# Attention and recurrence of a hybrid encoder layer: TensorE's order written out by the program

## The chip, the cores and the metric

The kernel runs on one core of a Trainium2 chip. The metric is the device time of one execution in microseconds (us). The core has five engines: TensorE (PE in the profile; its weight loads are listed as PEld), VectorE (DVE), ScalarE (ACT), GpSimd (POOL) and SyncE (SP, which here only issues DMA transfers). Each engine takes its own instructions strictly in the order of its queue; semaphores order the engines among each other.

## The reference

One layer of a streaming encoder over 1024 frames of width 1024, all in float32. Two mixers work on the same projection: chunked band attention (8 heads of 64) and a gated delta rule (4 heads of 128).

```python
u = rms_norm(h, mix_norm_gain);  proj = u @ w_in
aq, ak, av, dqkv, dgate, da, db = split(proj)
# A: own chunk of 64 frames and the 8 before it, QK-RMSNorm, learned bias on the distance
scores = einsum('bcqhd,bckhd->bchqk', qc, kb) * Dh**-0.5 + bias
o = einsum('bchqk,bckhd->bcqhd', softmax(scores), vb)
# B: gated DeltaNet: conv(4)+SiLU, L2-normalised q and k, chunked recurrence
t_mat = a_strict + eye(CHUNK)
value, k_cumdecay = solve(t_mat, v_beta), solve(t_mat, k_beta * exp(decay))
def step(S, inp):                          # S0 = 0
    v_new = val - kc @ S
    o = qd @ S + att @ v_new
    return S * cd + kt.T @ v_new, o
h = h + concat[rms_norm(A), rms_norm(B) * silu(dgate)] @ w_out
h = h + relu(rms_norm(h) @ w_ff1)**2 @ w_ff2
```

## The kernel before, in words

The program is written in a tile framework: it emits instructions with tiles, and a scheduler orders every engine's queue by a simulated timeline, with the order of emission as priority. Pools of tiles have a set number of buffers; a tile waits until one is free.

Stages, in order of time: projections (a 128x512 weight block times the transposed input, three passes of a split float32); attention and recurrence together; the output projection; two feed-forward products.

The recurrence works in chunks of 128 frames (NT = 8). `delta_prep` builds for each chunk the strictly lower matrix A and stores it (`a_dr`), stores `kt` for the state update, and inverts the 32x32 diagonal blocks of all chunks together by substitution on VectorE; the inverses go to `x_dr` and transposed to `y_dr`. For each chunk, `delta_merge` joins the inverted blocks: first 32 to 64 (tiles p1, p2, lines 568 and 577), then 64 to 128 (tp, p4, lines 582 to 594). `delta_state` makes the serial steps (c_tpv, c_pk, c_pv, c_pq, c_pS), `delta_out` the output within the chunk (c_Ltd, c_tpq, c_mt, c_po), `delta_fin` its transpose. The four-head products come from the helper on line 461, each float32 matmul of 128 columns as two instructions in the trace. `delta_all` deals the steps of neighbouring chunks out in the order of the string ORDER; each step ends with a `yield` of a cost.

Attention works on units (g, t, pp): a group g of four heads, a tile t of 128 queries, a pair pp of heads. A unit has up to n = 5 tiles of keys. `score` makes the products (t_sb for the last two key tiles, t_sa for the older ones, line 793) into three PSUM banks of pool ps_a, VectorE adds the bias and takes the maximum, ScalarE the exponential. `value` transposes the probabilities with PE (t_tpb line 844, then t_tpa line 855 for each of two heads) through the two banks of pool ps_t; ScalarE and VectorE copy them out (lines 847, 860, 858), and PE multiplies with the values (t_o, line 865). `finish` divides by the sums and `turn` transposes the result into `mix`.

The three generators `attention`, `delta_all` and the rest of the value projection (`values`) are dealt out by `interleave`, which always advances the one with the least work done by its weight. That sets only the order of emission, so the priority; where an instruction lands in PE's queue is the scheduler's choice, instruction by instruction.

Of the kernel before, what the change touches and what calls it, by code (L numbers as in the profile page):

```python
# [8 lines left out]
F32 = mybir.dt.float32  # L9
F32R = mybir.dt.float32r  # L10
AF = mybir.ActivationFunctionType
ALU = mybir.AluOpType
# [26 lines left out]
WARM = 8  # L39
LAST = {"b22": "t1", "t3": "t2", "t4": "b22"}  # L40
RS = "a"
NV = 6
# [4 lines left out]
def hymba_kernel(  # L47
# [60 lines left out]
    nc.gpsimd.memset(ones, 1.0)  # L108
    warm = bank(ps_o, "warm")
# [66 lines left out]
    def load_xt(hf, k):  # L176
# [9 lines left out]
        nc.vector.scalar_tensor_tensor(lo, raw, mgain[:, k:k + 1], hi.bitcast(F32), ALU.mult, ALU.subtract)  # L186
        acc = squares[hf][k % 2]
# [7 lines left out]
    for k in range(NKT):  # L195
        if k:
            w_dk.append(load_w(w_in[k * P:(k + 1) * P, DK:DK + 512], f"wdk_{k}"))
        load_xt(0, k)
        if not k:
            w_dk.append(load_w(w_in[0:P, DK:DK + 512], "wdk_0"))  # L200
# [30 lines left out]
    nc.gpsimd.memset(state[0], 0.0)  # L231
# [259 lines left out]
    def delta_prep(kT, ab):  # L491
# [4 lines left out]
        for c in range(NT):  # L496
# [5 lines left out]
            kt = page("pp", n + "_kt")  # L502
            nc.vector.tensor_tensor(b4(kt), b4(tp), bc_row(ab["edec"][:, 1, h4]), ALU.mult)
            nc.sync.dma_start(out=kt_dr[c], in_=kt)
# [45 lines left out]
    def delta_merge(c, res):  # L550

        n = f"m{c}"
        Ap, Yp, s1 = (page("pp", n + k) for k in ("_ab", "_yb", "_s1"))
        A, Y = b4(Ap), b4(Yp)
        X = s1[:, 384:512].rearrange("p (h e) -> p h e", h=4)
        Yc = s1[:, 256:384].rearrange("p (h e) -> p h e", h=4)
        nc.sync.dma_start(out=Ap, in_=a_dr[c])
        for dst, src in ((X, x_dr), (Yc, y_dr)):
            nc.sync.dma_start(out=dst, in_=src[4 * c:4 * c + 4].rearrange("b r h e -> (b r) h e"))
        nc.gpsimd.memset(Yp, 0.0)  # L560
        for b in range(4):
            bs = slice(32 * b, 32 * b + 32)
            nc.gpsimd.tensor_copy(Y[bs, :, bs], Yc[bs])
        yield 0
        p1 = bank(ps_d, n + "_p1")
        for c0 in (0, 64):
            for h in range(4):
                nc.tensor.matmul(p1[c0:c0 + 32, 32 * h:32 * h + 32], A[c0:c0 + 64, h, c0:c0 + 32],
                                 Y[c0:c0 + 64, h, c0 + 32:c0 + 64], start=True, stop=True)
            nc.scalar.copy(s1[c0:c0 + 32, 0:128], p1[c0:c0 + 32, 0:128])  # L570
        yield 500
        p2 = bank(ps_d, n + "_p2")
        for c0 in (0, 64):
            cs = slice(c0, c0 + 32)
            for h in range(4):
                hs = slice(32 * h, 32 * h + 32)
                nc.tensor.matmul(p2[cs, hs], X[cs, h, :], s1[cs, hs], start=True, stop=True)
            nc.scalar.mul(Y[cs, :, c0 + 32:c0 + 64], p2[cs, 0:128].rearrange("p (h e) -> p h e", h=4), -1.0)
        yield 500
        tp = bank(ps_d, n + "_tp")  # L580
        for h in range(4):
            nc.tensor.transpose(tp[0:64, h * 64:h * 64 + 64], Y[0:64, h, 0:64], ident[0:64, 0:64])
        for h in range(4):
            nc.tensor.matmul(tp[0:64, 256 + h * 64:320 + h * 64], A[64:128, h, 0:64], Y[64:128, h, 64:128],
                             start=True, stop=True)
        x1 = s1
        nc.scalar.copy(x1[0:64, :], tp[0:64, :])
        yield 700
        p4 = bank(ps_d, n + "_p4")
        for h in range(4):  # L590
            hs = slice(h * 64, h * 64 + 64)
            nc.tensor.matmul(p4[0:64, hs], x1[0:64, hs], x1[0:64, 256 + h * 64:320 + h * 64],
                             start=True, stop=True)
# [4 lines left out]
    def delta_state(c, ab, kTs, Ys, D):  # L598

# [8 lines left out]
        ktail = page("cv", n + "_kt")  # L608
        nc.sync.dma_start(out=ktail, in_=kt_dr[c])
# [5 lines left out]
        pk = bank(ps_d, n + "_pk")  # L615
        four(pk, lambda h, hs: kT[:, hs], lambda h, hs: S[:, h, :])
        for h in range(4):
            hs = slice(h * P, (h + 1) * P)
            nc.vector.scalar_tensor_tensor(
                rr[:, hs], pk[:, hs], ab["nbr"][:, 4 * c + h:4 * c + h + 1], rr[:, hs],  # L620
                ALU.mult, ALU.add)
        yield 900
# [6 lines left out]
        pq = bank(ps_d, n + "_pq")  # L629
        four(pq, lambda h, hs: dq[:, hs], lambda h, hs: S[:, h, :])  # L630
        o = page("cv", n + "_o")
        nc.vector.tensor_tensor(b4(o), b4(pq), bc_row(ab["edec"][:, 0, h4]), ALU.mult)
        yield 900
        pS = bank(ps_d, n + "_pS")
        four(pS, lambda h, hs: ktail[:, hs], lambda h, hs: vn[:, hs])
        for h in range(4):
            nc.vector.scalar_tensor_tensor(
                S2[:, h, :], S[:, h, :], ab["edec"][:, 2, 4 * c + h:4 * c + h + 1],
                pS[:, h * P:(h + 1) * P], ALU.mult, ALU.add)
# [3 lines left out]
    def delta_out(c, ab, kTs, D):  # L643
# [23 lines left out]
        nc.vector.tensor_tensor(o, o, po, ALU.add)  # L667
# [19 lines left out]
    def delta_all(ab, kTs):  # L687

        Ys, D = {}, {}
        merge = delta_merge(0, Ys)  # L690
        yield from merge
        merge = delta_merge(1, Ys)
        for c in range(NT + LATE):
# [3 lines left out]
            merge = delta_merge(c + 2, Ys) if c + 2 < NT else iter(())  # L697
# [8 lines left out]
    def attention(after):  # L706
# [50 lines left out]
        yield 0  # L757
# [650 lines left out]
```

## Time and profile before

| | |
|---|---|
| median of 3 runs | 1289.5 us (1288.38 to 1290.1) |
| the profiled execution | 1288.31 us, span 1286.6 us |
| granted TensorE clock | 0.998 |
| PE busy | 1260.6 us (98%), 6702 instructions |
| PEld busy | 1040.6 us (81%) |
| DVE, ACT, POOL busy | 935.0 us (73%), 553.9 us (43%), 293.0 us (23%) |
| DMA | 160.65 MB, mean 125 GB/s |

The span runs from the first to the last instruction of the program. The ends of matmuls are modelled by the profiler, and matmuls overlap, so a sum of their durations is longer than the time they take, and the busy share of PE is near 1 wherever they follow each other without a visible gap. The distance between two starts is measured. In a timeline, instructions of the same kind that follow each other are merged into one row with a count. Numbers at the ends of names are left out by the profile, so `t_sb` stands for that tile of all units.

### The profile page before, as it was taken

Reading aid. Unit: us, or ns where it says so; the run is one execution under the profiler, and the core shown is the slowest. Engines: PE = TensorE matmul, PEld = TensorE weight load, DVE = VectorE, ACT = ScalarE, POOL = GpSimd, SP = SyncE. Lnnn points to the kernel's source line nnn. Section 1 sums busy time; section 2 is a strip of 40 time slices with the busy share of each in tenths; the row PEclk is TensorE's granted clock in tenths of the full one; section 3 lists DMA queues with packets and bytes.
Section 4 is the critical chain, followed back from the end, with each engine's and each line's share of the span. In section 5 each row is a group of like instructions: output and inputs, shape, how many; then the busy total and the mean of one; then the engine's idle time right before and its main releaser. Section 6 shows DMA issues by size and latency. Waiting matters only on the chain.

```text
span 1286.6 us, 18043 instructions
## 1 busy us (share of the span) xinstructions
PE 1260.6 (98%) x6702; PEld 1040.6 (81%) x6702; DVE 935.0 (73%) x1401; ACT 553.9 (43%) x919; POOL 293.0 (23%) x499
## 2 busy tenths in 40 slices
PE   9999999999999999989999999999999999999998
PEld 7778878788888887868877788888887888888886
DVE  7899987665046666863529876776668997897988
ACT  7233132133166664665335445444455443333331
POOL 4435461454024355523310000000000000000034
PEclk9999999999999999999999999999999999999999
DMA  6214353656492742125351433232358733422002
GB/s 223 61 44 140 100 164 112 145 147 160 144 270 79 218 109 75 42 65 163 122 166 31 151 116 129 98 110 97 105 196 318 238 93 104 131 86 95 17 33 98
DMA packets 129288, 160.65 MB, mean 125 GB/s; under 512 B 22832, under 2 KB 71984, under 8 KB 128688
## 3 DMA queue, kind: packets, MB, share of 16 engines
q1 hardware_dynamic: 111104, 137.20, 34.7%
q10 hardware_dynamic: 18096, 22.29, 5.0%
q8 instruction: 53, 0.87, 0.3%
q14 instruction: 35, 0.29, 0.1%
HBM read 111.75 MB, written 47.71 MB: 124 GB/s over the span
## 4 chain that ended last, share of the span: by engine, by line
PE 72%; DVE 8%; issue 2%; DMA 2%; POOL 1%; ACT 1%; POOLq 1%; SPq 0%; ACTq 0%; DVEq 0%
PE q L1087 22%; PE p L1183 20%; PE op L166 5%; PE av_ps L166 3%; PE aq_ps L166 3%; PE g_ps L166 3%; PE t_o L865 3%; PE ak_ps L166 2%; PE t_sb L793 1%; PE t_sa L793 1%; PE t_tpb L844 1%; PE t_tpa L855 1%; PE c_mt L461 1%; PE c_pS L461 1%; DVE ml L148 1%
## 5 line engine op out<-in xcount | busy, mean ns | idle before, releaser
L1255 POOL TENSOR_TENSOR y<-y,y 128x1024 f32<-128x1024 f32 x6 | 19.3, 3243 | 591.7 <-DVE y L1251 572.9
L1251 DVE TENSOR_TENSOR y<-y,p 128x1024 f32<-128x1024 f32 x46 | 55.2, 1218 | 5.4 <-PE p L1183 4.5
L808 DVE CUSTOM_DVE_ANT_0 t_pb<-t_sb,biasn 128x256 f32<-128x256 f32 (+1 forms) x64 | 25.4, 402 | 43.6 <-POOL biasn L720 25.4
L166 PE MATMUL op<-mh,wo_h 128*128 128x512 f32 x128 | 50.3, 393 | 0.8 <-DVE t_nm L808 0.3
L166 PE MATMUL op<-ml,wo_h 128*128 128x512 f32 x128 | 50.1, 391 | 0.0
L166 PE MATMUL op<-mh,wo_l 128*128 128x512 f32 x128 | 48.3, 391 | 0.0
L823 ACT ACTIVATE t_pb<-t_pb,t_nm 128x256 f32<-128x256 f32 (+1 forms) x64 | 31.6, 494 | 22.7 <-DVE t_nm L817 12.7
L966 DVE TENSOR_TENSOR h<-op,op_x 128x512 f32<-128x512 f32 x16 | 10.8, 688 | 30.7 <-PE op L166 30.7
L793 PE MATMUL t_sb<-ks,t_q 128*128 128x256 f32 (+1 forms) x144 | 30.4, 308 | 0.8 <-DMA t_q<-q_dr 0.5
L973 POOL TENSOR_TENSOR op_q<-op_q 128x512 f32<-128x512 f32 x14 | 20.1, 1439 | 48.0 <-ACT op_q L972 47.8
L166 PEld LDWEIGHTS op<-mh,wo_h 128*128 128x128 f32 x128 | 24.0, 188 | 7.4 <-issue 1.0
L817 DVE CUSTOM_DVE_ANT_0 t_pa<-t_sa,biaso,t_nm 128x384 f32<-128x384 f32 (+2 forms) x48 | 26.3, 547 | 4.4 <-PE t_sa L793 2.9
L865 PE MATMUL t_o<-t_ta,vt 128*64 128x128 f32 x240 | 27.3, 293 | 1.4 <-DVE t_ta L858 1.1
L166 PEld LDWEIGHTS op<-mh,wo_l 128*128 128x128 f32 x128 | 24.0, 188 | 5.2 <-issue 0.2
L166 PEld LDWEIGHTS op<-ml,wo_h 128*128 128x128 f32 x128 | 24.0, 188 | 4.9
L166 PE MATMUL g_ps<-uh,wg_h 128*128 128x512 f32 x64 | 25.2, 394 | 1.4 <-ACT wg_h L147 1.4
L826 ACT ACTIVATE t_pa<-t_pa,t_nm 128x384 f32<-128x384 f32 (+2 forms) x48 | 26.4, 550 | 0.1
L793 PE MATMUL t_sa<-ks,t_q 128*128 128x256 f32 (+2 forms) x128 | 25.5, 310 | 0.3 <-DVE t_nm L808 0.3
L166 PE MATMUL g_ps<-uh,wg_l 128*128 128x512 f32 x64 | 25.2, 394 | 0.4 <-POOL wg_l L148 0.4
L166 PE MATMUL dq_ps<-uh,wdq_h 128*128 128x512 f32 x64 | 25.5, 398 | 0.0
L166 PE MATMUL dv_ps<-uh,wdv_l 128*128 128x512 f32 x64 | 25.4, 397 | 0.0
L166 PE MATMUL aq_ps<-waq_h,uh 128*128 128x512 f32 x64 | 25.3, 401 | 0.0
(1102 smaller groups left out, 4353.8 us busy)
## 6 DMA issues: line engine op xcount, KB each, us to landing
wa<-in_w_ff_dram SPq DMA_DIRECT2D x32, 512.0 KB
a<-in_w_ff_dram SPq DMA_DIRECT2D x32, 512.0 KB
b<-f_dr SPq DMA_DIRECT2D x32, 512.0 KB
f_dr<-yy ACTq DMA_DIRECT2D x16, 512.0 KB
t_q<-q_dr SPq DMA_DIRECT2D x30, 256.0 KB
f_dr<-zz ACTq DMA_DIRECT2D x13, 512.0 KB
ks<-k_dr SPq DMA_DIRECT2D x16, 256.0 KB
wo_r<-in_w_out_dram SPq DMA_DIRECT2D x16, 256.0 KB
```

What stands on the lines that cost most here:

```text
L166: nc.tensor.matmul(ps, a, b, start=(i == 0), stop=(i == n - 1))
L461: nc.tensor.matmul(ps[:, hs], lhs(h, hs), rhs(h, hs), start=True, stop=True)
L793: nc.tensor.matmul(o, q[m][:, i * P:(i + 1) * P], k[:, c], start=(m == 0), stop=(m == 1))
L808: nc.vector.tensor_tensor_reduce(sb[:, c], bk[:, c], new[g][pp][:, c], -1.0, 3.0e38, ALU.add, ALU.min, nm[:, 4 + i:5 + i])
L817: nc.vector.tensor_tensor_reduce(sa[e][:, 0:wa], bk[:, 0:wa], old[g][i][:, 384 - wa:384], -1.0, nm[:, 4 + i:5 + i], ALU.add, ALU.min, nm[: ...
L823: nc.scalar.activation(sb[:, c], sb[:, c], AF.Exp, bias=m, scale=-1.0, accum_out=T["sums"][:, 4 + i:5 + i])
L826: nc.scalar.activation(sa[e][:, 0:wa], sa[e][:, 0:wa], AF.Exp, bias=m, scale=-1.0, accum_out=T["sums"][:, i:i + 1])
L865: nc.tensor.matmul(po[64 * e:64 * e + 64, pp * P:(pp + 1) * P], vt[k0 + j][:, 64 * h:64 * h + 64], (ta[e] if j < na else tb)[:, c:c + P], ...
L973: nc.gpsimd.tensor_tensor(acc, acc, sq, ALU.add)
L1087: nc.tensor.matmul(part(ps, q), l[:, s], r, start=(k + m == 0), stop=(k == 3 and m == 2))
L1183: nc.tensor.matmul(part(ps[q], 0) if by_rows else part(ps[q // 2], q % 2), l[:, s], part(r, k), start=(i + k + m == 0), stop=(i + k + m == 4))
L1251: nc.vector.tensor_tensor(y[i][m], y[i][m], ps[m], op)
```

## The change

Four things change.

1. The attention's loop. `value` is cut into `flip` (transposes and copies) and `multiply`. A loop in `attention` now emits everything of this stage itself, also the steps of the recurrence and the value projection. It keeps a clock `now` of PE's planned time: a flip comes at least LS = 5000 ns after its score, a multiply LT = 2000 after its flip, finish 1200 after the last multiply of a tile, turn 8000 after finish, and recurrence steps at least LD = 300 apart, in step with the attention work done. The whole stage is emitted within `tc.manual_schedule` for PE: PE issues the stage's instructions in the order of emission. The other engines' order stays the scheduler's, and so does the place of instructions of PE that are emitted outside of it.
2. The first merges (32 to 64) are made for four chunks at once by `delta_low`, chunks 0 to 3 behind `delta_prep` in the projections, chunks 4 to 7 within the recurrence. It loads blocks with 32 small DMAs; `held` keeps a set of its matmuls together. `delta_merge` keeps the second merge.
3. The first chunk has no products with the zero state, and the last one makes no new state.
4. At the start: 11 instead of 8 warm matmuls (each two instructions in the trace), a ScalarE activation on `ones` ahead of the input's, and the first weights' load and split emitted between the input's split and its square.

```diff
-WARM = 8
+WARM = 11
+DELTA = 69e3
+AHEAD = 3
+LS, LT, LD = 5000, 2000, 300
+LAGS = 0.05
...
+    turn_on = cpool.tile([P, 1], F32, name="turn_on")
+    nc.scalar.activation(turn_on, ones[:, 0:1], AF.Square)
     warm = bank(ps_o, "warm")
...
         nc.vector.scalar_tensor_tensor(lo, raw, mgain[:, k:k + 1], hi.bitcast(F32), ALU.mult, ALU.subtract)
+        if not hf and not k:
+            w_dk.append(load_w(w_in[0:P, DK:DK + 512], "wdk_0"))
...
-    nc.gpsimd.memset(state[0], 0.0)
...
+    def held(args, step):
+        first = step(*args[0])
+        with tc.issue_after(first.ins), tc.high_priority():
+            for a in args[1:]:
+                step(*a)
+
+    def delta_low(b, W, tag):
+        n = f"l{b}"
+        W += [page("pp", f"{n}_w{i}") for i in range(2)]
+        xa, s1 = page(tag, n + "_xa"), page(tag, n + "_s1")
...
+        for c in range(4):
+            q = 16 * b + 4 * c
+            for k in range(4):
+                nc.sync.dma_start(out=Y[c // 2][32 * k:32 * k + 32, c % 2, :, 32 * (k % 2):32 * (k % 2) + 32],
+                                  in_=y_dr[q + k])
+            for r0 in (0, 64):
+                nc.sync.dma_start(out=XA[r0:r0 + 32, c], in_=x_dr[q + r0 // 32])
+                nc.sync.dma_start(out=XA[r0 + 32:r0 + 64, c], in_=a4[c, r0 + 32:r0 + 64, :, r0:r0 + 32])
+        yield 0
+        places = [(c, h, slice(128 * c + 32 * h, 128 * c + 32 * h + 32)) for c in (3, 2, 1, 0) for h in range(4)]
+        p1 = bank(ps_d, n + "_p1")
+        for r0 in (0, 64):
+            rs, rs2 = slice(r0, r0 + 32), slice(r0 + 32, r0 + 64)
+            held(places, lambda c, h, hs: nc.tensor.matmul(
+                p1[rs, hs], XA[rs2, c, h, :], Y[c // 2][rs2, c % 2, h, 32:64], start=True, stop=True))
+            nc.scalar.copy(s1[rs], p1[rs])
+        yield 1000
...
     def delta_state(c, ab, kTs, Ys, D):
...
+        if c:
+            pk = bank(ps_d, n + "_pk")
...
+        if c:
+            pq = bank(ps_d, n + "_pq")
...
+        if c + 1 < NT:
+            pS = bank(ps_d, n + "_pS")
...
+            if c == 2:
+                merge = chained(delta_low(1, W, "wh"), merge)
...
-        def value(g, t, pp):
+        def flip(g, t, pp):
...
+        def multiply(g, t, pp):
...
+        units = [(g, t, pp) for g in range(2) for t in range(NT) for pp in range(2)]
+        size = [min(t + 1, 5) for g, t, pp in units]
+        total = sum(664 * n + 390 for n in size)
...
+        while multiplied < len(units) or later or live:
+            later.sort(key=lambda p: p[0])
+            first = begun < len(units) and begun - multiplied < AHEAD and ("v" not in live or units[begun][1] < 2)
+            wants = "d" in live and now >= delta_at
+            if wants and deltas < DELTA * (spent / total - LAGS):
+                cost = fill(delta, "d")
+                now, deltas = now + cost, deltas + cost
+                delta_at = now + LD
+            elif multiplied < flipped and now >= ready[multiplied]:
+                g, t, pp = units[multiplied]
+                multiply(g, t, pp)
+                now += 218 * size[multiplied] + 240
+                spent += 218 * size[multiplied] + 240
+                if pp:
+                    later.append((now + 1200, 220, finish, (g, t)))
+                multiplied += 1
+            elif later and now >= later[0][0]:
+                _, cost, step, args = later.pop(0)
+                step(*args)
+                now += cost
+                if step is finish and args[0]:
+                    later.append((now + 8000, 440, turn, args[1:]))
+            elif flipped < begun and now >= ends[flipped] and flipped - multiplied < 2:
+                flip(*units[flipped])
+                now += 218 * size[flipped]
+                spent += 218 * size[flipped]
+                ready.append(now + LT)
+                flipped += 1
+            elif first:
...
+                score(g, t, pp)
+                now += 228 * size[begun] + 150
+                spent += 228 * size[begun] + 150
+                ends.append(now + LS)
+                begun += 1
+            elif "v" in live:
+                now += fill(values, "v")
...
-        (delta_prep(kT, ab), 0.35))
-    interleave((attention(after[NV - 1]), 1.0), (delta_all(ab, kT), 2.0), (values, WV))
+        (chained(delta_prep(kT, ab), delta_low(0, W, "pp")), 0.35))
+    with tc.manual_schedule(engines={mybir.EngineType.PE}):
+        attention(after[NV - 1], delta_all(ab, kT, W), values)
```

More of the change, by code (lines that the diff above doesn't have):

```diff
@@ L704, in delta_all, with attention @@
                 yield from gens[k]
-    def attention(after):
+    def attention(after, delta, values):
         def bias_page(tag, name):
@@ L1348, in hymba_kernel @@
     ab = ab_proj(u)
+    W = []
     after = []
```

171 lines of the change are left out of this document (88 added, 83 removed).

## The prediction

> **What bounds the kernel now.** I read the page's chain, then the busy time by stretch, then the groups of TensorE (PE) in the stretch that the change rewrites, and last PE's own timeline there. The page's chain, by engine:
> ```profile
> PE 72%; DVE 8%; issue 2%; DMA 2%; POOL 1%; ACT 1%; POOLq 1%; SPq 0%; ACTq 0%; DVEq 0%
> ```
> PE is the chain. By stretch (columns: stretch, length, then busy us and count of each engine), a projection and the attention with recurrence:
> ```profile
> 20.00:60.00 40.00, 40.00 (x197) 32.24 (x196) 33.93 (x56) 17.88 (x30) 17.56 (x18) 1.00 0.33 106
> 345.00:574.00 229.00, 220.32 (x2002) 186.74 (x2001) 142.97 (x441) 136.03 (x400) 93.33 (x258) 0.99 0.42 121
> ```
> In 345 to 574 us PE shows 220.32 of 229.00 us busy, so 8.7 us idle. But ends of matmuls are modelled in this profile, so "busy" does not mean well packed; only the distance from start to start tells. In the first row 197 instructions, mostly of 512 columns, fill 40 us, 0.203 us each. So I count what PE has to do between 345 and 574 us (groups of PE: count after the x, then busy us and mean ns of one):
> ```profile
> L793 PE MATMUL t_sb<-ks,t_q 128*128 128x256 f32 (+1 forms) x144 | 30.4, 308 | 0.8 <-DMA t_q<-q_dr 0.5 <-DVE t_nm L808 0.2
> L865 PE MATMUL t_o<-t_ta,vt 128*64 128x128 f32 x240 | 27.3, 293 | 1.4 <-DVE t_ta L858 1.1 <-ACT t_ta L860 0.2
> L793 PE MATMUL t_sa<-ks,t_q 128*128 128x256 f32 (+2 forms) x128 | 25.5, 310 | 0.3 <-DVE t_nm L808 0.3
> L865 PE MATMUL t_o<-t_tb,vt 128*64 128x128 f32 x240 | 23.4, 278 | 0.0
> L855 PE MATMUL t_tpa<-ident,t_pa 128*128 128x128 f32 x120 | 21.2, 282 | 1.1 <-ACT t_tb L847 1.1
> L844 PE MATMUL t_tpb<-ident,t_pb 128*128 128x128 f32 x120 | 20.0, 285 | 1.8 <-ACT t_on L893 0.9 <-DVE mixa L904 0.9
> L461 PE MATMUL c_pS<-c_vn,c_kt 128*128 128x128 f32 x64 | 9.2, 286 | 0.0
> ...
> L568 PE MATMUL m_p<-m_yb,m_ab 64*32 64x32 f32 x112 | 6.1, 195 | 0.3 <-ACT m_s L570 0.3
> L577 PE MATMUL m_p<-m_s 32*32 32x32 f32 x112 | 6.1, 194 | 1.4 <-ACT m_yb L578 0.8 <-DVE c5q_ss L488 0.5
> L887 PE MATMUL t_on<-ident,t_pb 128*128 128x128 f32 x30 | 5.9, 278 | 0.2 <-ACT t_pb L884 0.2
> L465 PE MATMUL c_tpq<-ident,c_jq 128*128 128x128 f32 x32 | 5.5, 285 | 0.0
> L584 PE MATMUL m_tp<-m_yb,m_ab 64*64 64x64 f32 x64 | 5.4, 224 | 0.0
> ```
> That is 272 of scores (L793), 480 of values (L865), 240 flips of probabilities (L844, L855), 384 of the recurrence (six groups of 64 like c_pS), 224 of the first merges, and in rows like the last three 150 more transposes, 160 of 64x64 and some 92 of 512 columns: 2002 in all. How fast each kind goes in a row, and how it goes when broken up, stands in PE's timeline (start, length to the modelled end, what, count):
> ```profile
> 407.13 0.88 PE L865 MATMUL t_o<-t_ta,vt 128*64 128x128 f32 x12
> 407.84 0.61 PE L865 MATMUL t_o<-t_tb,vt 128*64 128x128 f32 x8
> 408.38 0.51 PE L793 MATMUL t_sb<-ks,t_q 128*128 128x256 f32 x2
> ...
> 412.04 0.43 PE L865 MATMUL t_o<-t_ta,vt 128*64 128x128 f32 x2
> 412.40 0.61 PE L793 MATMUL t_sa<-ks,t_q 128*128 128x384 f32 x2
> 412.94 0.76 PE L865 MATMUL t_o<-t_ta,vt 128*64 128x128 f32 x9
> ...
> 415.84 0.60 PE L844 MATMUL t_tpb<-ident,t_pb 128*128 128x128 f32 x4
> 416.28 1.06 PE L461 MATMUL c_pv<-c_jv,m_yb 128*128 128x128 f32 x8
> 417.17 1.06 PE L461 MATMUL c_mt<-c_jq,kT 128*128 128x128 f32 x8
> ...
> 418.55 1.11 PE L793 MATMUL t_sa<-ks,t_q 128*128 128x256 f32 x8
> 419.50 0.52 PE L855 MATMUL t_tpa<-ident,t_pa 128*128 128x128 f32 x3
> ```
> Twenty of the values in a row take 408.38 - 407.13 = 1.25 us, 0.0625 each; two of them cut off take 0.36, 0.18 each. Eight scores in a row take 0.95, 0.119 each; two cut off take 0.54, 0.27 each. Transposes: 0.44 / 4 = 0.11. Recurrence: 0.89 / 8 = 0.111. So PE's order itself costs time, and the scheduler's order changes the kind of work every few tenths of a us.
>
> Work in a row: scores 272 x 0.125 (a few are 384 wide) = 34.0; values 480 x 0.0625 = 30.0; transposes (240 + 150) x 0.11 = 42.9; recurrence 384 x 0.111 = 42.6; first merges 6.1 + 6.1 = 12.2; the 64x64 at about their busy time, 14; 92 x 0.203 = 18.7. Sum 194.4. The stretch takes 229, so 34.6 us are idle (8.7) or lost to broken order (about 26).
>
> **The change part by part.**
>
> Order. PE issues score, flip, multiply and each step of the recurrence whole and in the plan's order; at best all 34.6 us come back. Nothing outside that list is added to PE there except the last two blocks of the value projection, which already lie in this stretch.
>
> First chunk and last chunk. Chunk 0 loses c_pk and c_pq, chunk 7 loses c_pS: 3 x 8 x 0.111 = 2.7 us of PE, on the path. Their work on VectorE (DVE) and the store and load of the last kt go too; DVE is busy 142.97 of 229 us, so I count nothing for those.
>
> First merges for four chunks. The old merge makes 32 such PE instructions a chunk, 256 in all; the new one makes 2 x 128, 256 again, in runs of 32 where there were runs of 8. I take 2 us off (bounds 0 and 5, from 12.2 us of busy time for 224 in runs of 8). Half of it moves ahead of this stretch into the projections, where PE is full as well, so the move earns nothing. On SyncE's queue (SP) the new form issues 32 loads for each four chunks and one per chunk later, 72 instead of 24. The same small loads of a_dr cost there now (ns, min/median/max):
> ```profile
> L531 SPq DMA_DIRECT2D ad<-a_dr x32: 262/352/399, 98.7 to 199.2; - x32
> ```
> So 32 x 0.352 = 11.3 us of SP before the second group, with loads of t_q queued behind. Their sources are stored in the projections already and two sets of pages are free, so they can be issued ahead of their place; I cost them at nothing; without that cover PE stands up to 11 us, once. GpSimd (POOL, busy 93.33 of 229) clears and copies less, the state's clear goes, and ScalarE (ACT) loses a few short copies; neither sets the end.
>
> The wait that fixed order adds. A flip is three groups of transposes (t_tpb, t_tpa, t_tpa) through two banks of ps_t, so the third waits until ACT has copied the first out. In two places it waits for that today, in the second with nothing between the groups:
> ```profile
> 553.20 0.37 PE L855 MATMUL t_tpa<-ident,t_pa 128*128 128x128 f32 x1 [0.79 <-ACT t_tb L847]
> ...
> 566.05 0.49 PE L855 MATMUL t_tpa<-ident,t_pa 128*128 128x128 f32 x3
> 566.89 0.33 PE L855 MATMUL t_tpa<-ident,t_pa 128*128 128x128 f32 x1 [0.35 <-ACT t_tb L847]
> ```
> At 566.05 three transposes take 0.33, the next starts after 0.84: 0.51 us lost with ACT free. At 553.20 ACT was in its exponentials and the copy came late: 0.79 idle, after four scores (0.5 in a row) that the scheduler had put between, so 1.3 without them. The flips with three groups are 2 x 6 x 2 = 24. Bounds 24 x 0.51 = 12.2 and 24 x 1.3 = 31; ACT is busy 136.03 of 229, and I take 0.75 each, nearer the free case: 18 us. Behind the waiting transposes stands everything on PE, that is the price.
>
> Other waits. Scores use three banks of ps_a, and two scores directly after each other wait for DVE: the plan has few, 2 us (0 to 5). The idle that stands now, 8.7, I leave in with 6 (3 to 12): recurrence steps whose input is late, and the tail. Units still change kind some 220 times: 2 us (0 to 5).
>
> Start. Three more warm matmuls, and a first ACT instruction without inputs that pulls the table load forward:
> ```profile
> 3.20 1.28 ACT L185 ACT_TABLE_LOAD   x1 [3.20 <-DMA mgain<-in_mix_norm_gain_dram]
> ```
> ```profile
> 1.05 3.78 PE L111 MATMUL warm<-ones 128*128 128x128 f32 x16 [1.05 <-POOL ones L108]
> 6.30 0.79 PE L307 MATMUL dk_ps<-uh,wdk_h 128*128 128x512 f32 x1 [1.47 <-ACT wdk_h L147]
> 6.89 0.63 PE L307 MATMUL dk_ps<-ul,wdk_h 128*128 128x512 f32 x1
> 7.32 0.63 PE L307 MATMUL dk_ps<-uh,wdk_h 128*128 128x512 f32 x1
> ```
> The inputs come at 3.20, the 1.28 us load is then done, and the weights' copy no longer stands behind the square. So the first product could start near 4.8; the warm ones, 22 instead of 16 records at about 0.22, end near 5.9, without the 1.47 us of idle. That is 0.4 us. The first products lie 0.43 apart against 0.203 later although the granted clock reads 1.00; if the unbroken start makes eight of them run at 0.203, that is 1.8 more. Bounds 0 and 3; I take 1.5. [...]
>
> Sum: 34.6 + 2.7 + 2 + 1.5 = 40.8 gained; 18 + 2 + 6 + 2 = 28 given back; net 12.8. The profiled execution took 1288.31 us (span 1286.6 and 1.7 around it), 1.2 below the median of 1289.5. 1288.3 - 12.8 = 1275.5; against the median 1276.7, so I say 1277.
>
> **The rivals.**
>
> Slower: the flip's wait decides. At 0.51 it costs 12.2, at 1.3 it costs 31. The sum turns at (40.8 - 10) / 24 = 1.28 us a flip. For it: PE is squeezed, so ACT's 136.03 us fall into a shorter stretch and its exponentials stand before the copy more often. Against it: the scheduler still orders ACT, and there is 40% of idle. At 1.6 us a flip: 38.4 + 10 - 40.8 = 7.6 slower, 1297.
>
> Same: late inputs. The recurrence has about 95 steps in fixed order; each that stands 0.13 us more eats the 12.8. For it: DVE works 142.97 us and would be busy three quarters of a stretch near 190. Against it: the plan puts one to two us of attention, by its own numbers, between most steps. Then 1289.
>
> Faster by much: the copies keep up, 0.51 a flip, and idle falls to 3: 40.8 - 12.2 - 3 - 1 = 24.6, so 1265.
>
> The order buys nothing, because PE is as full as it gets. Loads of weights (the second engine's column) are busy 186.74 / 229.00 = 0.815 in the stretch and 32.24 / 40 = 0.806 in a projection that runs at full pace. If that were the measure, only 2.7 + 2 + 1.5 = 6.2 would be gained and the flips' 12.2 lost: 6 slower, 1295. Against it: 0.0625 in a row and 0.18 cut off, for the same kind. [...]
>
> **How the numbers follow.** My forecast (1268 to 1286) gets 0.49, much faster (below 1268) 0.18, same 0.11, slower by the flips 0.18, PE already full 0.04. Within 0.2%, 2.6 us, about what a measurement of this kernel can tell from no change, is 1286.9 to 1292.1. So faster 0.67, same 0.11, slower 0.22. Range: low 1260, the fast case with its waits at their lower bounds (1289.5 - 29); high 1293, which leaves out about half of the slower cases and a little at the low end. The forecast's own range is 1268 to 1286.
>
> **What would show it.** In the changed profile the values should stand 16 to 20 in a row, at 0.0625; scores 8 to 12 in a row; the attention stretch should be near 215 us with about as much DVE and ACT work; waits of PE on t_tb L847 should be the largest, 24 of them; c_pk and c_pq should count 56; the first dk product should start near 6 with no idle before it and about 0.2 spacing. I am wrong if PE's waits there sum to over 40 us, if PE waits for the loads of the low merge, or if the spacing in a row is not kept.

## The result, and the profile after

The changed kernel took 1359.28 us (median of 4 runs, 1356.87 to 1364.4); before took 1288.94. The ratio is 1.0555, 95% interval 1.0519 to 1.059. The forecast was 1277, so it was wrong in sign and by 82 us. The profiled execution took 1364.4 us, 76.1 more than that of before.

The page of the changed kernel: the granted clock in 40 slices (before: only nines), and the chain by engine.
```profile
PEclk9999999999889978888999999999999999999999
...
PE 50%; DVE 5%; ACT 1%; issue 1%; POOL 1%; POOLq 0%; DMA 0%; ACTq 0%; DVEq 0%
```
The clock falls below nine tenths in slices 11 and 12 and again in 15 to 19 (each is 34 us long): that is the stage that the change rewrites. Where the 76 us went is seen by cutting the profile at two marks, the first product of the value projection and the first of the feed-forward part. Busy time by stretch (stretch, length, then busy us and count of PE, PEld, DVE, ACT and POOL, then the granted clock), before and after:
```profile
314.10:663.00 348.90, 338.90 (x2534) 282.86 (x2532) 184.35 (x497) 178.99 (x471) 126.23 (x288) 1.00 0.43 128
```
```profile
317.50:738.70 421.20, 350.40 (x2402) 294.40 (x2400) 180.55 (x485) 173.50 (x446) 122.81 (x278) 0.91 0.34 102
```
The stretch begins 3.4 us later and is 72.3 us longer; what follows it on PE takes 618.4 us in both. PE's idle in it rose from 10.0 to 70.8 us (length less busy). The other engines have as much to do as before; they are only spread over more time. What PE waited for:
```profile
PE t_sb L835 <- DVE t_nm L850: 29.2, 32, 2.0
PE t_tpa L894 <- ACT t_tb L886: 16.1, 22, 4.2
PE c_tpo L470 <- DVE c_o L714: 11.5, 1, 11.5
PE t_sb L835 <- DMA biasn<-in_rel_bias_dram: 4.6, 1, 4.6
PE c_pk L466 <- ACT m_sa L618: 3.1, 1, 3.1
```
Each row gives who waited, for whom, the sum in us, the number of waits and the longest. The second row is the flips' wait that the prediction named. The first, the largest, it had put at 2 us. There are 32 such waits, one for each score unit. In the timeline of all engines:
```profile
506.53 0.48 PE L835 MATMUL t_sb<-ks,t_q 128*128 128x256 f32 x2
506.60 0.69 DVE L646 TENSOR_TENSOR c_jv<-c_tpv,br 128x512 f32<-128x512 f32 x1
...
507.20 0.41 DVE L936 TENSOR_TENSOR t_on<-t_on,t_tot 128x256 f32<-128x256 f32 x1
507.53 0.41 DVE L850 CUSTOM_DVE_ANT_0 t_pb<-t_sb,biasn 128x256 f32<-128x256 f32 x1
...
508.01 0.50 PE L835 MATMUL t_sb<-ks,t_q 128*128 128x256 f32 x2 [1.00 <-DVE t_nm L850]
```
`score` writes the first head's t_sb into one half of a bank, has VectorE read it, and then writes the second head's into the other half of the same bank. The second product waits for the read, 1.00 us here, and the read stands behind two other instructions on DVE. The scheduler of before had put something between. Before, PE's timeline, from the middle of a passage that the prediction quotes (its two rows around these are 408.38, t_sb x2, and 412.04):
```profile
408.81 0.43 PE L568 MATMUL m_p<-m_yb,m_ab 64*32 64x32 f32 x8
409.18 0.55 PE L855 MATMUL t_tpa<-ident,t_pa 128*128 128x128 f32 x3
409.48 0.60 PE L793 MATMUL t_sa<-ks,t_q 128*128 128x384 f32 x2
409.92 0.49 PE L855 MATMUL t_tpa<-ident,t_pa 128*128 128x128 f32 x3
410.25 1.06 PE L461 MATMUL c_pk<-state,kT 128*128 128x128 f32 x8
411.24 0.43 PE L577 MATMUL m_p<-m_s 32*32 32x32 f32 x8
411.60 0.51 PE L793 MATMUL t_sb<-ks,t_q 128*128 128x256 f32 x2
```
From 408.38 to 411.60 the two heads' products stand apart, with six other pieces of work between. I had read such rows as broken order. They were, in part at least, the cover of a wait.

Two more rows are not in the list of waits. Stretches of 3.4 us, columns as above:
```profile
348.30:351.70 3.40, 3.35 (x16) 2.63 (x14) 0.00 (x0) 0.13 (x1) 0.00 (x0) 1.00 0.00 0
351.70:355.10 3.40, 0.00 (x0) 0.00 (x0) 0.00 (x0) 0.55 (x1) 1.25 (x10) 1.00 0.55 162
355.10:358.50 3.40, 1.76 (x7) 1.57 (x8) 0.90 (x6) 1.48 (x6) 0.40 (x2) 0.50 0.96 338
...
372.20:375.60 3.40, 3.40 (x23) 2.42 (x21) 0.00 (x0) 1.03 (x3) 0.18 (x1) 1.00 0.85 279
375.60:379.00 3.40, 2.13 (x17) 1.69 (x16) 1.99 (x11) 1.75 (x6) 0.00 (x0) 1.00 0.99 327
379.00:382.40 3.40, 3.02 (x21) 2.14 (x18) 1.11 (x6) 2.28 (x9) 0.00 (x0) 0.50 0.84 246
```
PE is idle in one stretch, or for 1.27 us of it, and the clock is 0.50 in the next. What that costs, PE's timeline, the same product in both clocks:
```profile
350.17 0.40 PE L172 MATMUL av_ps<-wav_l,uh 128*128 128x512 f32 x1
350.41 0.39 PE L172 MATMUL av_ps<-wav_h,ul 128*128 128x512 f32 x1
...
360.62 0.63 PE L172 MATMUL av_ps<-wav_l,uh 128*128 128x512 f32 x1
361.05 0.63 PE L172 MATMUL av_ps<-wav_h,ul 128*128 128x512 f32 x1
```
0.24 from start to start at 1.00, 0.43 at 0.50. In the stretch of the changed kernel the half clock holds for 78.5 us, of which PE works 59.2. I take half of that as lost, 29.6 us (by these two spacings it is 26); before it held for 3.4 us. The account of the stretch is then: before 348.8 = 337.1 of work at full clock + 10.0 idle + 1.7 lost to the clock; after 421.2 = 320.8 + 70.8 + 29.6.

### The profile page after: what moved, and what is told of

Read it like the earlier page. It is cut to its first block, busy times and chain, and to the rows that moved or that the text cites. A ratio compares the mean times of both kernels' runs of the same rounds, so it can differ in the third digit from the quotient of the medians.

```text
span 1362.7 us, 18037 instructions
## 1 busy us (share of the span) xinstructions
PE 1275.6 (94%) x6684; PEld 1055.3 (77%) x6684; DVE 931.4 (68%) x1388; ACT 551.4 (40%) x900; POOL 287.1 (21%) x486
## 4 chain that ended last, share of the span: by engine, by line
PE 50%; DVE 5%; ACT 1%; issue 1%; POOL 1%; POOLq 0%; DMA 0%; ACTq 0%; DVEq 0%
PE q L1180 20%; PE p L1276 19%; PE op L172 6%; POOLq L1498 0%; PE t_o L914 0%; DVE y L1348 0%; PE t_sb L835 0%; DMA wo_r<-in_w_out_dram 0%; PE t_sa L835 0%; DVE h L1121 0%; DVE y L1344 0%; PE c_po L466 0%; PE t_tpa L894 0%; ACT t_tb L886 0%; PE c_pv L466 0%
## 5 line engine op out<-in xcount | busy, mean ns | idle before, releaser
L835 PE MATMUL t_sb<-ks,t_q 128*128 128x256 f32 (+1 forms) x144 | 35.8, 348 | 33.8 <-DVE t_nm L850 29.2
L835 PEld LDWEIGHTS t_sb<-ks,t_q 128*128 128x128 f32 x144 | 24.6, 220 | 41.6 <-DVE t_nm L850 40.5
L894 PE MATMUL t_tpa<-ident,t_pa 128*128 128x128 f32 x120 | 23.2, 295 | 16.5 <-ACT t_tb L886 16.1
L897 DVE COPY t_ta<-t_tpa 128x384 f32<-128x384 f32 (+2 forms) x24 | 11.8, 490 | 35.0 <-PE t_tpa L894 35.0
L1059 DVE TENSOR_TENSOR h<-op,op_x 128x512 f32<-128x512 f32 x16 | 10.8, 686 | 33.1 <-PE op L172 33.1
L894 PEld LDWEIGHTS t_tpa<-ident,t_pa 128*128 128x128 f32 x120 | 13.9, 145 | 23.1 <-ACT t_tb L886 22.2
L172 PE MATMUL aq_ps<-waq_h,uh 128*128 128x512 f32 x64 | 25.5, 400 | 1.4 <-ACT waq_h L153 1.4
L172 PE MATMUL av_ps<-wav_h,ul 128*128 128x512 f32 x64 | 26.0, 407 | 0.0
L172 PE MATMUL av_ps<-wav_l,uh 128*128 128x512 f32 x64 | 26.0, 406 | 0.0
```

The costliest lines, as they stand in the source:

```text
L172: nc.tensor.matmul(ps, a, b, start=(i == 0), stop=(i == n - 1))
L835: nc.tensor.matmul(o, q[m][:, i * P:(i + 1) * P], k[:, c], start=(m == 0), stop=(m == 1))
L894: nc.tensor.transpose(tp[:, js], sa[e][:, js], ident)
L897: turned[1].append(nc.vector.tensor_copy(ta[e][:, 0:na * P], tp[:, 0:na * P]).ins)
```

## The experiments

All that follow are read by the same account, made from the starts on PE's timeline of one profiled execution each (us). "Idle" is the gaps that the profile shows; the rest of the stretch is work, and what of it lies in half clock counts half as work and half as lost. A wait shorter than the modelled end of a matmul hides in "work". The profiled executions of e6 and e17 were the fastest of theirs, by 6.7 and 3.1 us under the median. "Fixed" is the number of the 32 units within the fixed order.

| kernel | fixed | median | ratio to before (95%) | stretch | work at full clock | idle | lost to half clock |
|---|---|---|---|---|---|---|---|
| before | 0 | 1288.9 | 1 | 348.8 | 337.1 | 10.0 | 1.7 |
| changed | 32 | 1359.3 | 1.0519 to 1.059 | 421.2 | 320.8 | 70.8 | 29.6 |
| e1 paired products | 32 | 1314.4 | 1.017 to 1.0234 | 372.1 | 319.2 | 44.1 | 8.9 |
| e2 added work | 32 | 1357.3 | 1.0513 to 1.0553 | 416.0 | 341.6 | 53.6 | 20.8 |
| e3 scheduler's order | 0 | 1290.0 | 1.0002 to 1.0029 | 346.0 | 327.3 | 14.7 | 4.1 |
| e4 e1 + cut flips | 32 | 1303.3 | 1.0089 to 1.0135 | 362.9 | 316.9 | 32.3 | 13.6 |
| e5 e4 + values first + lead | 32 | 1303.2 | 1.0108 to 1.0139 | 358.4 | 316.6 | 35.0 | 6.8 |
| e6 e1 + lead | 32 | 1340.1 | 1.0375 to 1.0426 | 392.9 | 319.8 | 49.8 | 23.4 |
| e7 before + start | 0 | 1287.2 | 0.9988 to 1.0005 | 348.8 | 337.6 | 11.2 | 0.0 |
| e8 e7 + dropped products | 0 | 1310.9 | 1.0168 to 1.0196 | 372.7 | 338.4 | 24.7 | 9.6 |
| e9 e4 + values first | 27 | 1289.2 | 0.9999 to 1.0023 | 348.7 | 319.0 | 24.6 | 5.1 |
| e10 the same, long distances | 32 | 1296.6 | 1.0038 to 1.0072 | 353.7 | 315.5 | 28.6 | 9.6 |
| e12 e3 + paired products | 0 | 1283.3 | 0.9941 to 0.9971 | 338.4 | 323.9 | 12.8 | 1.7 |
| e13 as e9 | 12 | 1281.4 | 0.9934 to 0.997 | 341.3 | 320.7 | 14.6 | 6.0 |
| e14 as e10 | 24 | 1282.7 | 0.9946 to 0.9975 | 341.3 | 318.0 | 15.3 | 8.0 |
| e15 as e10, merges earlier | 20 | 1279.9 | 0.9924 to 0.9958 | 334.0 | 317.8 | 12.9 | 3.4 |
| e16 as e10 | 12 | 1275.5 | 0.9886 to 0.9915 | 336.6 | 320.2 | 11.2 | 5.2 |
| e17 emission of e10 | 0 | 1284.6 | 0.9964 to 0.9984 | 338.7 | 320.0 | 14.7 | 4.0 |
| e18 as e16, merges earlier | 12 | 1276.1 | 0.9891 to 0.9935 | 335.6 | 320.5 | 11.8 | 3.4 |

**e1, paired products.**
```diff
             for e in range(2):
-                cost += product(g, T, i, bk, c.start, kb, t + 1)
-                nc.vector.tensor_tensor_reduce(sb[:, c], bk[:, c], ...)
+                cost += product(g, T, 2 * pp + e, bk, e * 256 + 256 - wb, kb, t + 1)
+            for e in range(2):
+                nc.vector.tensor_tensor_reduce(sb[:, c], bk[:, c], ...)
```


> The changed kernel with one edit: in a score unit the products of both heads into the shared bank (t_sb) are emitted first, then VectorE's two reads. In the changed kernel TensorE waits 32 times, 29.2 us in all, for the read of the first head before it may write the second head's half of the same bank. Theory (the fixed order exposes this alternation): the waits of PE on t_nm go from 29.2 to under 6 us, part of the half-clock time goes with them, and the time falls from 1359 to 1310 to 1330 us. Rival (VectorE is simply behind, the wait only shows where it is met first): the waits move to t_sa and the flips, and the time stays within 10 us of the changed kernel, 1349 to 1362.

Measured 1314.4. What PE waits for:
```profile
PE t_tpa L895 <- ACT t_tb L887: 14.7, 22, 2.0
PE c_tpo L470 <- DVE c_o L714: 11.0, 1, 11.0
...
PE t_sb L835 <- DVE t_nm L851: 2.9, 3, 1.4
```
The order of emission it was: 32 waits became 3, 29.2 us became 2.9, the flips' waits and the one at the end stayed, and 21 us of half-clock loss went too. Two moved lines are worth 45 us.

**e2, work in the place of idle.**
```diff
+                if e and wa:
+                    for _ in range(4):
+                        nc.tensor.matmul(idle[:, 0:P], ones, ones, start=True, stop=True)
                 cost += product(g, T, i, bk, c.start, kb, t + 1)
```


> The changed kernel with work added: in each of the 24 score units that have old keys, four products of ones with ones (128 columns, f32, into a bank that is overwritten right after) stand between the first and the second head's t_sb, where TensorE waits for VectorE some 0.9 us. That is 96 instructions, 192 records at about 0.11 us, 21 us of work in the place of about 22 us of idle; nothing is taken away. Theory (idle gaps make the array's clock fall to half, and that costs on top of the waits): the half-clock time between 345 and 652 us falls from 78 us to under 40, and the kernel with more work is faster than the changed kernel by 8 to 20 us, 1339 to 1351. Rival (the low clock has another cause or costs nothing): the time is the same or longer, 1359 to 1380.

Measured 1357.3: both numbers of the theory missed, and the time is nearer the rival's. The half clock fell only from 78.5 to 54.6 us, and 17 waits stayed:
```profile
PE t_sb L835 <- DVE t_nm L854: 11.0, 17, 1.4
```
Nine of them, 5.2 us, stand in units that got the added products; seven stand in the eight units without old keys, which got none, and one ahead of a first head. In the stretch, 20.8 us of work were added and 17.2 of idle filled, 3.6 more if the clock cost nothing; it became 5.2 shorter, and the loss to the half clock 8.8 smaller. That speaks for the theory; the medians differ by 2.0 with overlapping ranges and settle nothing alone. What shows the price is the spacing above, 0.43 against 0.24.

**e3, the order undone** (`with tc.manual_schedule(...)` taken away, all else as changed).

> The changed kernel with TensorE's order left to the scheduler again; the plan still sets the order of emission, and the first merges for four chunks, the dropped products and the start stay. Theory (the fixed order alone made it slower): 1270 to 1290 us, the waits of PE on t_nm under 8 us, hardly any half clock. Rival (the plan's emission or the merges for four chunks are what is slow): it stays above 1310.

Measured 1290.0, 0.02 to 0.29% above before, at the theory's upper end. So the fixed order made the loss. Its largest wait is another one:
```profile
PE t_sb L835 <- DMA t_q<-q_dr: 5.2, 2, 4.8
```

**e4, flips cut in two.** In the plan's loop the third group of transposes becomes a step of its own:
```diff
                 for e in range(2):
+                    if e:
+                        yield
                     tp = bank(ps_t, f"{n}_tpa{i}")
...
+            elif half and now >= half[0]:
+                for _ in half[1]:
+                    pass
...
+                    half = now + 900, turns
```


> The kernel with both heads' products ahead of VectorE's reads, and beside it the flip cut in two: the third group of transposes (t_tpa of the second head) is a step of its own at least 900 ns of the plan later, so that other work stands where TensorE waits for ScalarE's copy of t_tb (16.1 us in 22 waits in the changed kernel). Theory (the wait is one of order, other work can stand there): the waits of t_tpa on t_tb fall from 16 to under 5 us, and the time is 8 to 18 us under the kernel with the paired products alone. Rival (ScalarE is late as such): the wait moves to other instructions, and the time is within 4 us of it.

Measured 1303.3, 11.1 less than e1, and the wait is gone:
```profile
PE t_tpa L897 <- ACT t_tb L887: 1.9, 3, 0.7
```

**e5 and e6, the recurrence leads** (`LAGS = -0.05` for 0.05), in e5 on e4 with one block of the value projection ahead of the loop, in e6 on e1.

> The kernel with paired products and flips cut in two (1303), and two more edits of the plan: one block of the value projection stands before the first score, where TensorE waited 3.4 us at 355 us, and the recurrence leads the attention's share of work by 0.05 where it lagged by 0.05 (LAGS), so that it isn't last. Theory (what is left is single places where the plan has no cover): the wait of c_tpo on c_o (3.5) and that of av_ps (3.4) go, the half-clock time falls from 31 us to under 20, and the time comes to 1286 to 1297. Rival (ScalarE, VectorE and GpSimd are late everywhere once TensorE's order is fixed): the waits move and the time stays 1299 to 1308.

> The kernel with the paired products (1314) with one more edit: the recurrence leads by 0.05 where it lagged by 0.05. There TensorE waits 11.0 us at 581 us for c_o of the recurrence's seventh chunk, whose chain stands on GpSimd's and ScalarE's queues behind splits of the output weights that wait for their loads. Theory (the recurrence is last in the plan, and nothing is left to stand there): the 11 us wait falls under 4 and the time falls by 6 to 14 us, to 1300 to 1308. Rival (the chain is held by the queues wherever it stands): the wait stays within 3 us of 11, and the time too.

Neither theory held. In e5 the value block covered its place (no idle ahead of the first scores), but c_tpo's wait grew from 3.5 to 8.2, and the time is that of e4. In e6 that wait fell from 11.0 to 6.4 and the time rose by 26: idle rose by 6 and the half-clock loss by 15, with waits on VectorE's maxima where e1 had few:
```profile
PE t_sa L835 <- DVE t_nm L860: 8.7, 8, 2.9
...
PE t_sa L835 <- DVE t_nm L851: 5.9, 6, 1.4
```
In this pair, then, what moving the recurrence did elsewhere outweighed the wait at the end. That wait's chain in the changed kernel, GpSimd's timeline:
```profile
635.76 1.26 POOL L154 TENSOR_TENSOR wo_l<-wo_r,wo_h 128x512 fp32r<-128x512 f32 x1 [3.76 <-ACT wo_h L153]
637.11 0.52 POOL L137 TENSOR_SCALAR c_v<-c_ss 128x4 f32<-128x4 f32 x1
```
The recurrence's c_v stands behind a split of the output weights that waits 3.76 us.

**e7 and e8, the other parts on the kernel before.** e7: 11 warm products, ScalarE's first instruction, the weights' load moved. e8: beside that, `if c:` around c_pk and c_pq, `if c + 1 < NT:` around c_pS and kt.

> The kernel before with the start alone: 11 warm products for 8, ScalarE's first instruction without inputs, and the first dk weights' load and split moved ahead of the square. The prediction took 1.5 us; in the changed kernel the first dq product starts at 59.9 where it stood at 61.2. Theory: 1.0 to 1.6 us faster, 1286.2 to 1286.8. Rival (the scheduler's order downstream shifts by more than that): anything within 3 us of before, with the gain at the first dq product still there.

> The kernel before with the start and with the three products of zero or unused state dropped (c_pk and c_pq of chunk 0, c_pS of chunk 7, with their work on VectorE, the kt store and load and the state's clear); first merges and order as before. Theory (each is worth its place on TensorE's path, 1.3 and 24 x 0.111 = 2.7): 1283 to 1285. Rival (dropped products only move the idle time): 1286 to 1288, like the start alone.

e7: 1287.2; the interval holds the expected 0.1% and zero. The first dq product starts at 60.4 where it stood at 61.2. e8 missed both theories: 24 instructions fewer on PE than e7 and 23.7 us slower, with 13.5 us more idle and 9.6 lost to the clock. I take it that `interleave` deals the remaining steps out in another order and the scheduler then arrives at another result; that is argued, not shown. What a dropped product is worth by itself can't be read from this run. It also shows by how much a small edit can move the time where the scheduler orders PE, and so how far one pair of such kernels can be trusted.

**e9, e10, e12, e13: the end, the distances, the pairs.** e9 and e13 close the fixed order after 27 and 12 units; e10 has longer distances; e12 is e3 with the edit of e1.
```diff
+        now += fill(values, "v")
         while multiplied < len(units) or later or live:
+            if multiplied == 27:            # 12 in e13
+                fixed.close()
...
-LS, LT, LD = 5000, 2000, 300                # e10, all 32 units fixed
+LS, LT, LD = 7000, 3000, 600
```


> The kernel with paired products and cut flips (1303), with one block of the value projection ahead of the first score, and the fixed order ended after 27 of the 32 units; from there the scheduler orders TensorE again and may put the output projection between. Theory (at the end the plan has nothing to put where c_tpo waits for c_o, and idle there also halves the clock): no wait over 3 us after 560 us, and 8 to 13 us less than 1303, so 1290 to 1295. Rival (the chain of the seventh chunk is late on GpSimd and ScalarE whatever order TensorE has): the wait stays at 3 us or more, 1299 to 1306.

> The kernel with paired products, cut flips and one value block ahead of the first score, and longer distances in the plan: score to flip 7000 for 5000, flip to multiply 3000 for 2000, recurrence steps 600 for 300. Theory (the distances are too short for the lateness of the other engines): the sum of TensorE's waits between 345 and 610 us falls by over 10 us and the time to 1288 to 1297. Rival (three units and two flips in flight are all that may be open, so longer distances leave the plan with nothing to issue): 1303 to 1320.

> The changed kernel with TensorE's order left to the scheduler (1290) and both heads' products emitted ahead of VectorE's reads. Theory (the scheduler had already put other work between the two heads, the alternation costs only under a fixed order): 1287 to 1293. Rival (the alternation costs in any order): 1275 to 1284.

> As the kernel whose fixed order ends after 27 units, but it ends after 12 of 32. Theory (each stretch in fixed order saves TensorE work and gives more back in idle and half clock): between the free order (1290) and 1303, at 1292 to 1298. Rival (the fixed order is a gain where the value projection and many units are at hand, and a loss only later): 1280 to 1288.

e9: 1289.2, 14.1 under e4 and just under the theory's range; c_tpo's wait is 2.3. But e9 also has the value block first, and e4's 3.4 us wait ahead of the first scores, with 6.8 us of half clock, is gone with it. What the early end gave by itself is not shown. e10: 1296.6, at the theory's upper end, but not by its cause: PE's idle between 345 and 610 us fell from 30.0 in e4 to 27.4, where the theory had over 10. One wait of 8.3 us is left, up to 575.8, and from 571.5 on the clock is at half for 10.2 us.
```profile
PE c_tpo L470 <- ACT wo_h L153: 8.3, 1, 8.3
```
e12 went against its theory: 1283.3, faster than e3 by 6.7. The alternation had a cost under the scheduler as well: from start to start at full clock, t_sb and t_sa take 39.1 us of work in e12 and 43.2 in e3. e13 too: 1281.4, in its rival's range. Against the free order of e3 that is 8.6 us less, but e3 lacks the paired products. Against e12, which has them, it is 1.9 less, and the intervals of the two overlap.

**e14 to e18, both together, and what the fixed order is worth.** They join the distances with an early end: after 24 (e14), 20 with `if c == 1:` for `if c == 2:` ahead of `delta_low` (e15), and 12 units (e16). e17 has the emission of e10 and no fixed order; e18 is e16 with the earlier `delta_low`.

> Paired products, cut flips, a value block ahead of the first score, the longer distances (7000, 3000, 600), and the fixed order ended after 24 of 32 units. Theory (the fixed order gains where distances cover the other engines' lateness, and the loss was at the end): the 8.3 us wait at the end and the half clock behind it go, 1297 comes down by 12 to 20, to 1277 to 1285, and the kernel with the shorter fixed stretch of 12 units isn't faster than this one. Rival (every longer stretch in fixed order loses): 1286 to 1292, slower than at 12 units.

> As the kernel with longer distances, but fixed for 20 units, and the first merges of the second four chunks are asked for one chunk earlier, where TensorE waited 1.4 to 2.3 us for their loads and copies and ran at half clock for up to 10 us around 440 us. Theory (single uncovered places): no half clock between 430 and 460 us, 1274 to 1282. Rival (the loads of the first merges then hold those of t_q, or idle moves elsewhere): 1282 to 1290.

> The longer distances with the fixed order ended after 12 of 32 units, where the short distances gave 1281. Theory (distances help in any length of the fixed stretch): 1276 to 1281. Rival (every stretch in fixed order loses, and with 12 units there is little of it left): 1281 to 1286, and faster than at 24 units.

> The same emission as the fastest kernel (paired products, cut flips, value block first, distances 7000, 3000, 600), with TensorE's order left to the scheduler throughout. Theory (the first stretch in fixed order gains, by whole runs of values and scores): 1279 to 1287, slower than 1275.5 by over 3. Rival (the gain is that of the emission alone): 1271 to 1277.

> The fastest kernel (fixed for 12 units, long distances) with the first merges of the second four chunks asked for one chunk earlier; in the fastest kernel TensorE waits 3.7 us at 441 us for the load of t_q, whose queue those merges' loads share, and runs 6.8 us at half clock after it. Theory (asked for earlier, those loads are out of the way): that wait and that half clock go, 3 to 7 us less, 1268 to 1273. Rival (the loads hold another t_q instead, or the wait stays): 1274 to 1279.

e16 is the fastest: 1275.5, ratio 0.9886 to 0.9915. Its stretch, and its order at work:
```profile
315.60:652.20 336.60, 325.36 (x2402) 275.64 (x2400) 176.27 (x485) 169.29 (x446) 125.13 (x278) 0.98 0.42 126
```
```profile
394.25 1.11 PE L835 MATMUL t_sb<-ks,t_q 128*128 128x128 f32 x8
395.20 0.92 PE L835 MATMUL t_sa<-ks,t_q 128*128 128x384 f32 x4
395.95 0.60 PE L884 MATMUL t_tpb<-ident,t_pb 128*128 128x128 f32 x4
396.39 0.49 PE L897 MATMUL t_tpa<-ident,t_pa 128*128 128x128 f32 x3
396.71 1.06 PE L466 MATMUL c_pq<-state,c_jq 128*128 128x128 f32 x8
397.70 0.66 PE L917 MATMUL t_o<-t_ta,vt 128*64 128x128 f32 x8
```
Whole runs of each kind, and no idle between them. e17 answers the question behind these runs: the same emission without the fixed order takes 1284.6, 9.1 us more, so for this emission fixing 12 units gains. Its stretch:
```profile
317.20:655.90 338.70, 324.03 (x2382) 274.77 (x2380) 175.60 (x485) 170.28 (x445) 124.83 (x275) 0.98 0.42 125
```
The theory's cause, whole runs of values and scores, is not borne out. Values do take 35.7 us in e16 for 37.5 in e17, but the recurrence's products take 42.1 for 40.7 and scores 38.3 for 38.6. All work at full clock is 320.2 us for 320.0, and the stretches differ by only 2.1 us, by less idle in e16. (The profiled executions differ by 5.0; the other 2.9 lie before and behind the stretch.) So the work that e16 has less of than before came with the emission, under either order, and where the rest of the 9.1 comes from is open. With 24 fixed units in place of 12, work falls by 2.2 us, but idle rises by 4.1 and the clock's loss by 2.8. So the theory of e14 held in its time and failed in its comparison with 12 units. e15's kept (no half clock between 430 and 460 us). e18's did not: the wait for t_q went, others of 2.2 and 1.8 us came, and the time is that of e16.

## Why the prediction was wrong

- **The failed step** is in "Other waits": "two scores directly after each other wait for DVE: the plan has few, 2 us (0 to 5)". I looked between units, where three banks give room, and not within one, where the emission has product, read, product, read on one bank. It is 29.2 us in 32 waits, and more hides behind modelled ends; taking it away was worth 45 us with its clock (e1). The prediction's own quoted rows showed two heads' t_sb apart, and counted this as loss.
- **The half clock** had no term. Idle was priced at its length; in the changed kernel 70.8 us of it brought 29.6 more. I had thought of the clock for the start alone. The row at 375.60 has 1.27 us of idle among 17 instructions, two gaps of 0.63 in the main, and in the row behind it, at 379.00, the clock is at 0.50.
- **"Order", 34.6 us**, of which about 26 for broken order, was over-sized. Work at full clock fell by 16.3 in the changed kernel and by 21.6 in e10, whose waits are fewer; in both are 2.7 of dropped products and about 7 of first merges, of which 3 only moved ahead of the stretch. That leaves some 12 for order in e10. From start to start at full clock, values take 30.8 us there for 38.0 before, scores 36.5 for 43.5. In the changed kernel values take 30.7, so that part came as forecast, but scores take 42.3 and the flips 33.1 for 29.3. The groups of e10 that answer to the prediction's rows (t_o 27.3 and 23.4 busy, c_pS 9.2 for 64):
```profile
L917 PE MATMUL t_o<-t_tb,vt 128*64 128x128 f32 x240 | 19.6, 285 | 0.0
L917 PE MATMUL t_o<-t_ta,vt 128*64 128x128 f32 x240 | 19.1, 291 | 0.0
...
L466 PE MATMUL c_pS<-c_vn,c_kt 128*128 128x128 f32 x56 | 7.9, 284 | 0.5 <-DVE c_ss L493 0.5
```
  c_pS takes 0.141 each, busy, for 0.144. From start to start the flips take 0.126 each in e10 for 0.122 before, and the recurrence's products 0.121 for 0.118. So the 774 transposes and recurrence products stood in runs already, and pricing them at their best spacing booked a gain that wasn't there.
- **The flips, 18 (12.2 to 31)**: 16.1 in 22 waits, 0.73 each where I took 0.75. Right, and curable (e4).
- **Other idle, 6 (3 to 12)**: 70.8 less 29.2 and 16.1 leaves 25.5, of which 11.5 is the end of the recurrence and 4.6 the bias at the first score; in before the value and output projections stood beside both. The plan had nothing to put there. Put together for the stretch, in the terms of the sum: work was to fall by 28.6 and fell by 16.3, idle was to rise by 17.3 and rose by 60.8, and the clock, at nothing, cost 27.9 more.
- **Start, 1.5**: the first dq product starts at 59.9 for 61.2, 1.3 earlier. The changed kernel's first dk products, PE's timeline:
```profile
1.05 5.07 PE L117 MATMUL warm<-ones 128*128 128x128 f32 x22 [1.05 <-POOL ones L112]
5.76 0.77 PE L312 MATMUL dk_ps<-uh,wdk_h 128*128 128x512 f32 x1
...
7.07 0.39 PE L312 MATMUL dk_ps<-ul,wdk_h 128*128 128x512 f32 x1
7.29 0.39 PE L312 MATMUL dk_ps<-uh,wdk_h 128*128 128x512 f32 x1
```
  No idle ahead of the first product, and 0.22 between the fourth and the fifth, where 0.43 lay between products before. I had read a granted clock of 1.00 there. That was no reading: the trace's first record of the clock begins at 10.64 us in before and at 6.92 in the changed kernel, and the spacing falls from 0.43 to 0.23 at just these times. That eight products would come to the closer spacing was an estimate: from 6.89 to 9.88 us before has seven spacings of 0.42 to 0.43, and the changed kernel has one, from 6.33 to 6.76. First merges: in the stretch they take 7.0 us less, and 3.2 of that is paid in the projections, where their first half now stands. From dq to the value projection the changed kernel takes 4.7 us more (257.6 for 252.9); the other kernels with these projections take from 254.8 to 257.8.
- **Signs that held**: values 20 in a row, 56 of c_pk. I had written that waits over 40 us would make me wrong; they did. None of my rivals had this mechanism: the slower one needed 1.28 us a flip.
- **Within reach**: e16 took 1275.5, about what I forecast, but by other sizes and in part by another cause: 16.9 less work, 1.2 more idle, 3.5 more lost to the clock. As e17 has the same work without a fixed order, the agreement with the forecast does not speak for its mechanism.

Open: what the fixed order gives beside the emission, and why 12 fixed units do better than 20 or 24. The account shows idle and clock rising with the length, not which engine's lateness makes it.

## What to carry to other kernels

Before you fix an engine's order, list for every unit the write, read, write on one buffer: what a scheduler puts between two such steps can be cover and not disorder, and a step must be emitted so that it needs none. Price idle of TensorE at its length and its clock, and price a gain from order kind by kind against rows of the same kind, not at the best spacing of all. Fix the order only where other work is at hand, and end it ahead of the tail. Try the new emission with the scheduler's order too, or its gain is put down to the fixed order.

## What the runs showed of the hardware

In the traces of before and of the changed kernel the granted clock changes in steps of 3.41 us: in the changed kernel its pieces from 355.08 to 648.63 us last 3.41 (the shortest, of which the others are whole multiples), 6.83, 10.24, 13.65, 17.07, 27.31, 34.13, 37.55 and 78.51 us. A window with partial idle was at times followed by half clock. Over the stage from 345 to 665 us in before, changed and the 17 other kernels above, counted in windows of that length on the trace's own grid that start there: after a window at full clock with less than 0.68 us of idle, none of 1428 was followed by half clock; with 0.68 to 1.36, 14 of 164; with 1.36 to 2.04, 23 of 49; above that, 23 of 23. At half clock, a window with less than 0.34 us of idle brought full clock back in 58 of 71, one with more in 2 of 46. (Idle here is what the modelled ends leave.) So a window of these runs did not have to be idle throughout for half clock to follow: 37 of the 60 that it followed had at most 2.04 us of idle.
